# Weight groups of a three-mixer decoder layer in another order, two more weight buffers, another PSUM bank for the narrow group

## The chip, the cores and the metric

The kernel runs on one core of a Trainium2 chip. The metric is the device time of one execution in microseconds (us), the median of the runs. TensorE (PE in the profile) multiplies, VectorE (DVE), ScalarE (ACT) and GpSimd (POOL) do the rest, and SyncE (SP) issues nearly all DMAs from one queue, in the order in which they were written.

## What is computed

One layer of a decoder runs over 288 token columns: 256 of a prompt and 32 of eight short decode sequences. Everything is float32.

```
m = silu(c) @ w_ada + b_ada;  shift, scale, gate = split(m, 3)
h = rmsnorm(x, g_norm) * (1 + scale) + shift
u_a, v_a, z_a, qkv_b, z_b, a_b, b_b, q_c, k_c, v_c, z_c, qi, ki, wi = split(h @ w_in)
y_a = chunk_mlp(gelu(u_a), layernorm(gelu(v_a))) * silu(z_a)      # gMLP
y_b = rmsnorm(gated_delta(conv(qkv_b), a_b, b_b)) * silu(z_b)     # delta rule
y_c = sparse_attention(q_c, k_c, v_c, qi, ki, wi) * silu(z_c)
x = x + gate * (concat(y_a, y_b, y_c) @ w_out);  y = rmsnorm(x, g_final)
```

`D_MODEL` is 4096. `w_ada` (4096 x 12288), `w_in` (4096 x about 15000) and `w_out` (4096 x 4096) are each read once.

## The kernel before

**Groups and units.** `w_in` is cut into 29 groups of 512 columns and one narrow group `c` of 112 columns; `w_out` has 8 groups. `group` makes a list of `Gemm` units of one group, one unit for each 128 rows of the contraction (`kk`). A unit multiplies its 128 x 512 weights with the 128 x 288 tile of h, in four column tiles, each into a PSUM bank of its own (`acc0` to `acc3`, from `acc_tile`). The narrow group has one tile and so used `acc0` alone. To keep float32 accuracy each weight tile is split into `wh` (a cast on ACT) and `wl` (a subtraction on DVE), and h into `hH` and `hL`; each tile of a unit is three matmuls, hH·wh, hL·wh and hH·wl. A full group is 32 units of 12 matmuls, 384 in all; the narrow one 96.

**Loads.** One DMA of 512 KB brings the raw weights of two `Gemm` units into one of four buffers `w` (`N_RAW`). The modulation `m` comes from `Ada` units; each of the first 128 takes two DMAs of 512 KB into buffers `wa` (`N_ADA`, five of them), and eight small matmuls `ada`. The loads stand on SP's queue in the order of the units that need them, so a load that waits for a free buffer holds back all loads behind it.

**First stage.** h isn't known until shift and scale are. `STEPS` cuts the 32 row blocks of h into six steps of two blocks and five of four. In each step the `Ada` units of the next step run between the `Gemm` units of this one; when a step's `ada` sum is complete, `ada_fin1` copies it (`adasb`), transposes it, adds the bias and calls `make_h`, which makes `htmp`, `hH` and `hL`. The groups of the first stage (`SG`: the narrow one, five of attention, and those that `PLAN["p1"]` names) go through all eleven steps, so each step's products are added into SBUF by DVE (`part_finish`; the rows `zb<-zb,acc`). The loop over `lb` spreads `Ada` units among `Gemm` units by a rate that lets each step's `ada` be complete `LEAD` units past its need; for the last step there is nothing past it, so its last `Ada` pair stands directly before its first `Gemm` unit. In a step of two blocks the before has 24 units and a rate of 0.4 `Ada` units each, in the steps 1 to 5; in a step of four 48 units and a rate of 1/3, in the steps 6 to 8.

**Second stage.** `ph2` lists the other groups: those of `PLAN["attn"]`, then the twelve of the delta rule's q, k and v (`C_QKV`), then those of `PLAN["dn3"]`, then v and u of the gMLP (`C_VA`, `C_UA`), then `w_out`. One of the 64 `Ada` units of `gate` stands after every eighth unit. Here h is whole: a gate group (`z_group`) goes from PSUM through `z_fin` into DRAM (`zD`), in one go. The mixers' own chains are Python generators (`dn_all`, `prompt_attn`, `gmlp_prep`, `mix_gen` and others); the `Weaver` puts their instructions between matmuls by its own estimate of times, and `W.finish` writes out all that is left of a chain where the code needs it done. Two such places matter here. `gmlp_open`, before unit 12 (`GMO`) of the last u group, finishes `DN[3]`, the delta rule's fourth and last chain. `need_mix`, before each fourth `w_out` unit of the first output group, finishes `MIX[kb]`: a load `mx` of finished mixer rows from DRAM (`mixD`), its cast `mH` on ACT and its rest `mL` on DVE. The `w_out` units use the K blocks in the order `KB = [2, 3, 4, 5, 6, 7, 0, 1]`; `mixD_160` is block 2, `mixD_165` block 7.

Of the kernel before, what the change touches and what calls it, by code (L numbers as in the profile page):

```python
# [36 lines left out]

GCOL = [512 * i for i in range(22)] + [C_QC + 512 * i for i in range(7)]
FULL = [(0, 128), (128, 128), (256, 128), (384, 128)]
N_RAW, N_ADA, N_SPLIT = 4, 5, 4  # L40
N_BANK = 4
HOP = 0.22
LEAD = 6
BACKLOG = 2.0
CALM = 2.5
NH = 3
LEAD0 = 0
GMO = 12
PAIR = 2
GATE = 8  # L50
GATE0 = 0
GPAIR = 1
STEPS = [(2 * f, 2) for f in range(2 * NH)] + [(4 * f, 4) for f in range(NH, 8)]
PLAN = {"p1": ["zc0", "zc1", "zb0", "zb1", "zb2", "zb3"], "attn": ["za0", "za1"], "dn3": []}


def _size(ap):
# [324 lines left out]
def tile_hybrid_step(ctx: ExitStack, tc: tile.TileContext, I, O):  # L382
# [63 lines left out]
    def w_in(c0):  # L446
        return I["w_in_t"][GCOL.index(c0)]
# [9 lines left out]
    def acc_tile(j):  # L457
        t = psum.tile([P, 512], F32, tag=f"acc{j}", name=f"acc{j}", bufs=1)
        W.bank_use[t.tensor.name] = ("T", 0.0)
        return t  # L460

    class Gemm(Unit):
# [21 lines left out]
        def mm(self, j):  # L484
            us = [self.with_, self] if self.with_ else [self]
            if j == 0 and us[0].first:
                self.st.acc = {}
            off, m = self.tiles[j]
            if us[0].first:
                self.st.acc[j] = acc_tile(j)  # L490
            acc = self.st.acc[j]
            for u in us:
                kk = u.kk
                xh, xl = self.XH[kk // 4][:, kk % 4], self.XL[kk // 4][:, kk % 4]
                a, b = u.wh[:, off:off + m], u.wl[:, off:off + m]
                T.matmul(acc[:m, :NTOK], a, xh, start=u.first, stop=False)
                T.matmul(acc[:m, :NTOK], a, xl, start=False, stop=False)
                T.matmul(acc[:m, :NTOK], b, xh, start=False, stop=u.last)
            if self.last:
                self.finish(j, acc)  # L500
# [265 lines left out]
    def make_h(k0, n):  # L766
# [19 lines left out]
        for c in range(0, n, 2):  # L786
# [12 lines left out]
          ("qc0", w_in(C_QC), FULL), ("qc1", w_in(C_QC + 512), FULL)]  # L799
    SG += [(n, w_in(ZCOL[n][0]), FULL) for n in PLAN["p1"]]  # L800

# [50 lines left out]
    la, lb, la_end = [], [], []  # L852
# [11 lines left out]

    at_, n = [0], la_end[0] + LEAD0
    for us in lb:
        at_.append(at_[-1] + len(us))
    W.units += la[:n]
    i = 0
    while i < len(lb):  # L870
        rate, nxt = max([((min(len(la), la_end[j] + LEAD) - n) / (at_[j] - at_[i]), j) for j in range(i + 1, len(lb))],
                        default=(0, len(lb)))
        us = [u for x in lb[i:nxt] for u in x]
        n0 = n
        for j, u in enumerate(us):
            e = min(len(la), n0 + int(rate * (j + 1)) // PAIR * PAIR)
            W.units += [u] + la[n:e]
            n = e
        i = nxt
# [1337 lines left out]
    def z_group(n):  # L2217
        return group(w_in(ZCOL[n][0]), FULL, ALL, z_fin(ZCOL[n][1]))
# [21 lines left out]
    ph2 = []  # L2240
    for n in PLAN["attn"]:
        ph2 += z_group(n)
    for g in range(4):
        for kind in range(3):
# [5 lines left out]
            ph2 += u  # L2250
    for n in PLAN["dn3"]:
        ph2 += z_group(n)
# [24 lines left out]
    for n in range(2):  # L2277
        u = group(w_in(C_UA + 512 * n), FULL, LAST if n else ALL, uv_finish(UT, 4 * n, y_gen if n else None))
        if n:
            u[GMO].pre.append(gmlp_open)  # L2280
            for i, kb in enumerate(KB[:6]):
# [4 lines left out]
    mixed, n = [], 0  # L2286
    for i, u in enumerate(ph2):
        e = min(len(gates), int((i + 1 - GATE0) / GATE)) // GPAIR * GPAIR
        mixed += [u] + gates[n:e]
        n = max(n, e)  # L2290
# [157 lines left out]
```

## Time and profile before

| | us |
|---|---|
| median of 3 runs | 2605.29 |
| lowest and highest | 2603.06 and 2607.48 |
| the profiled execution | 2601.98 |
| its span, first to last instruction | 2600.3 |
| PE busy | 2498.2 (96%) |
| DVE, ACT, POOL busy | 1622.6, 1055.8, 478.0 |

The first product of h starts at 52.69 us, the second stage at 789 us, the first output group at 2144 us and the last product ends at 2580 us. A matmul's own duration in the trace (about 300 ns) is longer than the distance between two starts, since they are pipelined; the distance is what counts. PEclk is the granted share of TensorE's clock: 1.00 is 2.4 GHz, 0.50 is 1.2 GHz.

### The profile page before, as it was taken

The numbers are of one execution on the slowest core, as the hardware profiler recorded it, in microseconds if no ns is written. First come the engines' busy times: TensorE is split into PE (matmuls) and PEld (weight loads), VectorE is DVE, ScalarE is ACT, GpSimd is POOL, SyncE is SP. The second block draws the span as 40 slices with busy tenths as digits, with TensorE's granted clock in tenths as the row PEclk, the third lists the DMA queues.
The fourth block names the chain that finished last, engine by engine and source line by source line (L and its number), as shares of the span: only waits on it lengthen the run. The fifth ranks groups of instructions, "written<-read, shape, count | busy, mean of one in ns | idle before, by whom it ended". The sixth has DMA issues, their size and how long they took to land. (4 is left out here: it accounts for less than half of the span.)

```text
span 2600.3 us, 51897 instructions
## 1 busy us (share of the span) xinstructions
PE 2498.2 (96%) x19572; PEld 2232.4 (86%) x19572; DVE 1622.6 (62%) x3616; ACT 1055.8 (41%) x2446; POOL 478.0 (18%) x1096
## 2 busy tenths in 40 slices
PE   5999999999999999999999999999999998999997
PEld 3788888888897788888899889989989988999997
DVE  3377765555568798555576576667567566555554
ACT  3423223323344434344444444444454534444443
POOL 1000000000001122534533333443330200000000
PEclk9999999999999999999999999999999999999998
DMA  7988988887656567877776565666666455555554
GB/s 281 369 328 340 343 321 316 314 326 298 220 182 207 169 224 255 284 255 259 252 261 204 171 224 204 203 218 222 200 219 236 143 198 163 188 173 177 177 186 162
DMA packets 207947, 615.88 MB, mean 237 GB/s; under 512 B 41901, under 2 KB 61841, under 8 KB 207697
## 3 DMA queue, kind: packets, MB, share of 16 engines
q1 hardware_dynamic: 196816, 574.82, 62.7%
q0 software_dynamic: 10880, 37.76, 4.2%
q8 instruction: 154, 2.52, 0.4%
q14 instruction: 97, 0.79, 0.1%
HBM read 587.54 MB, written 24.95 MB: 236 GB/s over the span
## 5 line engine op out<-in xcount | busy, mean ns | idle before, releaser
L74 DVE TENSOR_TENSOR wl<-w,wh 128x512 fp32r<-128x512 f32 (+1 forms) x1216 | 801.3, 682 | 672.9 <-ACT wh L74 662.9
L74 ACT CAST wh<-w 128x512 fp32r<-128x512 f32 (+1 forms) x1216 | 712.0, 611 | 1131.7 <-PE acc L74 816.0
L74 PE MATMUL acc<-hH,wh 128*128 128x288 f32 (+1 forms) x3744 | 1151.7, 308 | 20.2 <-ACT hH L74 8.7
L74 PE MATMUL acc<-hH,wl 128*128 128x288 f32 (+1 forms) x3744 | 1109.2, 296 | 1.4 <-DVE wl L74 1.3
L74 PE MATMUL acc<-hL,wh 128*128 128x288 f32 (+1 forms) x3744 | 1109.2, 296 | 0.6 <-DVE hL L74 0.6
L74 PEld LDWEIGHTS acc<-hH,wh 128*128 128x128 f32 (+1 forms) x3744 | 707.0, 189 | 137.7 <-issue 72.1
L74 PEld LDWEIGHTS acc<-hH,wl 128*128 128x128 f32 (+1 forms) x3744 | 708.0, 189 | 5.1 <-DVE wl L74 5.1
L74 PEld LDWEIGHTS acc<-hL,wh 128*128 128x128 f32 (+1 forms) x3744 | 708.5, 189 | 1.3 <-DVE hL L74 1.2
L74 PE MATMUL acc<-mH,wh 128*128 128x288 f32 x1024 | 304.6, 297 | 7.5 <-ACT mH L74 7.5
L74 PE MATMUL acc<-mL,wh 128*128 128x288 f32 x1024 | 302.6, 296 | 0.8 <-DVE mL L74 0.8
L74 PE MATMUL acc<-mH,wl 128*128 128x288 f32 x1024 | 302.8, 296 | 0.0
L74 PEld LDWEIGHTS acc<-mH,wh 128*128 128x128 f32 x1024 | 192.9, 188 | 8.0 <-ACT mH L74 7.7
L74 PEld LDWEIGHTS acc<-mL,wh 128*128 128x128 f32 x1024 | 193.0, 188 | 1.1 <-DVE mL L74 1.1
L74 PEld LDWEIGHTS acc<-mH,wl 128*128 128x128 f32 x1024 | 193.0, 189 | 0.0
L74 PE MATMUL ada<-wa,cT 128*32 128x512 f32 x1024 | 135.3, 608 | 23.9 <-DVE bs L74 18.0
L74 DVE TENSOR_TENSOR zb<-zb,acc 128x288 f32<-128x288 f32 x160 | 70.3, 451 | 43.3 <-PE acc L74 43.0
L74 PEld LDWEIGHTS ada<-wa,cT 128*32 128x32 f32 x1024 | 28.4, 110 | 80.3 <-issue 44.1
L74 POOL TENSOR_TENSOR htmp<-yT,gaT 128x32 f32<-128x32 f32 x20 | 7.8, 388 | 449.0 <-ACT wh L74 335.3
L74 POOL TENSOR_SCALAR frs<-frs 128x1 f32<-128x1 f32 (+1 forms) x3 | 0.9, 297 | 456.0 <-DVE frs L74 455.9
L74 DVE TENSOR_TENSOR R<-R,R 128x248 f32<-128x248 f32 (+30 forms) x248 | 72.7, 293 | 10.4 <-DMA R<-dD 3.9
L74 POOL DMA_INDIRECT vraw<-in_cache_v_dram,ixv x64 | 66.4, 1038 | 42.1 <-issue 13.9
L74 DVE SCALAR_TENSOR_TENSOR cv<-xp,vecs,cv 128x256 f32<-128x256 f32 x144 | 70.9, 492 | 3.6
(443 smaller groups left out, 2342.3 us busy)
## 6 DMA issues: line engine op xcount, KB each, us to landing
w<-in_w_in_t_dram SPq DMA_DIRECT2D x464, 512.0 KB, 4.7
wa<-in_w_ada_t_dram SPq DMA_DIRECT2D x256, 512.0 KB, 6.1
w<-in_w_ada_t_dram SPq DMA_DIRECT2D x128, 512.0 KB, 5.7
w<-in_w_out_t_dram SPq DMA_DIRECT2D x128, 512.0 KB, 3.5
St<-in_state_dn_t_dram SPq DMA_DIRECT2D x16, 512.0 KB, 6.2
out_dram<-St SPq DMA_DIRECT2D x16, 512.0 KB, 3.7
X<-in_x_prompt_dram SPq DMA_DIRECT2D x8, 512.0 KB, 7.1
XF<-in_x_prompt_dram SPq DMA_DIRECT2D x16, 256.0 KB, 5.2
```

What stands on the lines that cost most here:

```text
L74: r = f(*a, **k)
```

## The change

```diff
-N_RAW, N_ADA, N_SPLIT = 4, 5, 4
+N_RAW, N_ADA, N_SPLIT = 4, 7, 4
...
+LAST_LEAD = 8
...
-PLAN = {"p1": ["zc0", "zc1", "zb0", "zb1", "zb2", "zb3"], "attn": ["za0", "za1"], "dn3": []}
+PLAN = {"p1": ["zc0", "zc1", "zb0", "zb1"], "attn": ["zb2", "zb3"], "dn3": ["za0", "za1"]}
...
             if us[0].first:
-                self.st.acc[j] = acc_tile(j)
+
+                self.st.acc[j] = acc_tile(j if len(self.tiles) > 1 else 2)
...
-        rate, nxt = max([((min(len(la), la_end[j] + LEAD) - n) / (at_[j] - at_[i]), j) for j in range(i + 1, len(lb))],
+        rate, nxt = max([((min(len(la), la_end[j] + LEAD) - n) /
+                         (at_[j] - at_[i] - (LAST_LEAD if la_end[j] == len(la) else 0)), j) for j in range(i + 1, len(lb))],
```

Five things change. The first stage has two full groups fewer (`zb2`, `zb3`). They take the place of `za0`, `za1` in front of the delta rule's columns, and `za0`, `za1` (the gMLP's gate) now stand behind the delta rule's columns, in front of v and u. There are seven buffers `wa`. The narrow group accumulates in `acc2`. The last `Ada` pair of the first stage stands eight `Gemm` units earlier. A step of two blocks now has 20 units with 0.48 `Ada` units each (steps 1 to 5), a step of four 40 with 0.4 (steps 6 to 8), so 9.6 and 16 in a step as before.

The order of the instructions shows three of the places. First ACT at the end of the first stage's tenth step, where `hH` of the eleventh is made. Before:

```order
L74 CAST wh<-w 128x112 x4
L74 CAST wh<-w 128x512 x44
L74 CAST wh<-w 128x112 x4
L74 COPY adasb<-ada 128x512
L74 CAST hH_8112<-htmp 128x576 x2
L74 CAST wh<-w 128x512 x26
```

And now:

```order
L75 CAST wh<-w 128x112 x4
L75 CAST wh<-w 128x512 x32
L75 COPY adasb<-ada 128x512
L75 CAST wh<-w 128x512 x4
L75 CAST wh<-w 128x112 x2
L75 CAST hH_6878<-htmp 128x576
L75 CAST wh<-w 128x112 x2
L75 CAST hH_6878<-htmp 128x576
L75 CAST wh<-w 128x512 x26
```

The copy `adasb` has moved ahead of eight weight casts, so units of the tenth step now stand between it and `hH`. On PE, 84 products of the tenth step stand behind the transposes of this `adasb`, where none did.

Second, DVE at the end of the delta rule's last chain; `St` are the states of four heads, `Sup` the products that update them, `oTs` the transposed output. Before, all of it in one piece in front of the gMLP's first instruction (`rep`):

```order
L74 TENSOR_SCALAR R_26175<-R_25755,bsel 128x128 x8
L74 TENSOR_TENSOR wl<-w,wh 128x512
L74 TENSOR_SCALAR R_25755<-R_25755,onr 128x128
L74 SCALAR_TENSOR_TENSOR R_25755<-oTs,vecs,R_25755 128x128
L74 SCALAR_TENSOR_TENSOR St_24190<-St_24190,gls,Sup 128x128 x4
L74 SCALAR_TENSOR_TENSOR St_24191<-St_24191,gls,Sup 128x128 x4
...
L74 SCALAR_TENSOR_TENSOR St_24192<-St_24192,gls,Sup 128x128 x4
L74 SCALAR_TENSOR_TENSOR St_24193<-St_24193,gls,Sup 128x128 x4
L74 COPY rep<-ident 4x32
L74 TENSOR_TENSOR wl<-w,wh 128x512 x3
```

And now:

```order
L75 TENSOR_SCALAR R_24776<-R_24325,bsel 128x128 x8
L75 TENSOR_TENSOR wl<-w,wh 128x512 x2
L75 TENSOR_SCALAR R_24325<-R_24325,onr 128x128
...
L75 SCALAR_TENSOR_TENSOR St_22889<-St_22889,gls,Sup 128x128 x4
L75 TENSOR_TENSOR wl<-w,wh 128x512 x2
L75 SCALAR_TENSOR_TENSOR St_22888<-St_22888,gls,Sup 128x128 x4
L75 SCALAR_TENSOR_TENSOR St_22889<-St_22889,gls,Sup 128x128 x4
L75 TENSOR_TENSOR wl<-w,wh 128x512 x2
L75 SCALAR_TENSOR_TENSOR St_22890<-St_22890,gls,Sup 128x128 x4
L75 SCALAR_TENSOR_TENSOR St_22891<-St_22891,gls,Sup 128x128 x4
L75 TENSOR_TENSOR wl<-w,wh 128x512
```

Weight splits now stand between the state updates, and the gMLP's first instruction comes 750 products of PE behind the last `Sup`.

Third, SP around the start of `w_out`, from the loads of the last u group on. Before:

```order
L74 DMA w<-in_w_in_t_dram 128x1024 x4
L74 DMA w<-in_w_out_t_dram 128x1024
L74 DMA mx<-mixD_160 128x1152
L74 DMA w<-in_w_out_t_dram 128x1024
L74 DMA mx<-mixD_161 128x1152
L74 DMA w<-in_w_out_t_dram 128x1024 x5
L74 DMA out_dram<-vtk 32x1024
L74 DMA mx<-mixD_163 128x1152
L74 DMA w<-in_w_out_t_dram 128x1024 x3
L74 DMA mx<-mixD_162 128x1152
```

And now:

```order
L75 DMA mx<-mixD_161 128x1152
L75 DMA w<-in_w_in_t_dram 128x1024
L75 DMA w<-in_w_out_t_dram 128x1024
L75 DMA mx<-mixD_162 128x1152
L75 DMA w<-in_w_out_t_dram 128x1024 x7
L75 DMA out_dram<-vtk 32x1024
L75 DMA w<-in_w_out_t_dram 128x1024
L75 DMA mx<-mixD_163 128x1152
L75 DMA z_26712<-zD_151 128x288
L75 DMA w<-in_w_out_t_dram 128x1024 x2
L75 DMA z_26838<-zD_151 128x288
L75 DMA w<-in_w_out_t_dram 128x1024
```

Block 4 (`mixD_162`) has moved ahead of eight loads of `w_out` and of block 5 (`mixD_163`); block 5 stands about as many loads down the queue as block 4 did. In PE's order the product that needs block 4 is 194 products behind its load now and 0 before; the one that needs block 5 is 64 behind; the one that needs block 6 is 45 and most of 12 `mix` products behind its load.

## Rows read from the trace of the kernel before

**Rows 1.** The page's first section: busy us of each engine (share of the span).

```profile
PE 2498.2 (96%) x19572; PEld 2232.4 (86%) x19572; DVE 1622.6 (62%) x3616; ACT 1055.8 (41%) x2446; POOL 478.0 (18%) x1096
```

**Rows 2.** Stretches, tile `acc`: us, PE (count), PEld, DVE, ACT, PEclk, DMA share, GB/s.

```profile
112.41:350.08 237.67, 188.55 (x1351) 180.76 (x1351) 98.36 (x225) 0.00 (x0) 1.00 0.88 336
350.08:622.40 272.32, 224.73 (x1621) 216.82 (x1621) 59.33 (x135) 0.00 (x0) 1.00 0.83 318
...
711.90:722.00 10.10, 9.25 (x36) 8.58 (x37) 0.45 (x1) 0.00 (x0) 0.50 0.30 105
2107.43:2111.30 3.87, 3.23 (x9) 2.32 (x9) 0.00 (x0) 0.00 (x0) 0.51 0.61 243
2168.42:2176.00 7.58, 5.42 (x18) 4.41 (x18) 0.00 (x0) 0.00 (x0) 0.50 0.62 207
```

**Rows 3.** Stretches, all instructions; POOL's column comes ahead of PEclk.

```profile
30.00:40.00 10.00, 7.51 (x50) 3.40 (x48) 1.38 (x2) 2.04 (x9) 0.00 (x0) 0.97 0.90 302
70.00:130.00 60.00, 58.49 (x420) 45.67 (x417) 25.46 (x56) 30.39 (x68) 4.07 (x16) 1.00 0.95 368
```

**Rows 4.** PE's waits in the first stage: total us, times, longest.

```profile
PE acc L74 <- DVE v_c L74: 7.4, 7, 1.4
PE ada L74 <- DMA wa<-in_w_ada_t_dram: 1.2, 2, 1.0
```

**Rows 5.** DVE's timeline, end of a step (start, us, what, [idle before <-releaser]).

```profile
703.44 0.46 DVE L74 TENSOR_TENSOR zb<-zb,acc 128x288 f32<-128x288 f32 x1 [0.34 <-PE acc L74]
```

**Rows 6.** PE's timeline at the last step's start.

```profile
703.91 0.29 PE L74 MATMUL acc<-hH,wl 128*128 128x288 f32 x1
704.13 1.93 PE L74 MATMUL ada<-wa,cT 128*32 128x512 f32 x16
706.76 0.66 PE L74 MATMUL ada<-ident,adasb 128*128 128x128 f32 x4 [0.70 <-ACT adasb L74]
711.90 0.58 PE L74 MATMUL acc<-hH,wh 128*112 128x288 f32 x1 [4.48 <-ACT hH L74]
...
716.31 0.58 PE L74 MATMUL acc<-hH,wh 128*128 128x288 f32 x1 [0.64 <-DVE v_c L74]
```

**Rows 7.** PE's timeline at the last delta-rule chain's end, and `Sup` at 1896.

```profile
2095.67 0.29 PE L74 MATMUL acc<-hL,wh 128*128 128x288 f32 x1
...
2096.20 0.29 PE L74 MATMUL acc<-hH,wl 128*128 128x288 f32 x1
2099.67 0.33 PE L74 MATMUL oTs<-ident,R 128*128 128x128 f32 x1 [3.18 <-DVE R L74]
2099.93 7.57 PE L74 MATMUL Sup<-R,R 32*128 32x512 f32 x16
2107.43 0.61 PE L74 MATMUL acc<-hH,wh 128*128 128x288 f32 x1
...
1896.55 1.13 PE L74 MATMUL Sup<-R,R 32*128 32x512 f32 x4
```

**Rows 8.** Timelines of PE, SP and DVE where `w_out` begins.

```profile
2160.63 0.29 PE L74 MATMUL acc<-mH,wl 128*128 128x288 f32 x1
2168.42 0.61 PE L74 MATMUL acc<-mH,wh 128*128 128x288 f32 x1 [7.50 <-ACT mH L74]
2169.81 0.61 PE L74 MATMUL acc<-mL,wh 128*128 128x288 f32 x1 [0.79 <-DVE mL L74]
...
2155.84 6.74 SPq L74 DMA_DIRECT2D w<-in_w_out_t_dram  x3
2162.63 0.43 SPq L74 DMA_DIRECT2D mx<-mixD  x1
...
2168.40 1.36 DVE L74 TENSOR_TENSOR mL<-mx,mH 128x1152 fp32r<-128x1152 f32 x1 [3.78 <-ACT mH L74]
```

**Rows 9.** The tile `mx`: duration ns min/median/max; issue to landing.

```profile
L74 ACT CAST mH<-mx x6: 1133/1152/1157, 2136.7 to 2182.0; 128x1152 fp32r<-128x1152 f32 x6
...
DMA to landing us min/median/max: 3.6/5.5/6.3
```

## Prediction, made before the changed kernel was run

> **What bounds the kernel now.** I read the page first: PE is busy for 2498.2 us, 96% of the span [rows 1], so the reader should take PE as the bound and look for the time in which it stands still or runs slowly. The change leaves the number of products as it is; it can gain only from such time. The stage table tells what a product costs: five products start in 2095.67 to 2096.20, four distances in 0.53 us, 0.133 us each [rows 7]. The steps 1 to 5 of the first stage hold 1350 products (five times 270), or 179.6 us, in 237.67 us, and 48 Ada units, so one of these costs 1.21 us with all that comes with it; the steps 6 to 8 hold 1620 products and 48 Ada units in 272.32 us, which gives 1.18 [rows 2]. I use 1.2. The waits and timelines then show four kinds of lost time: short waits for `v_c` [rows 4], a wait for `hH` [rows 6], a wait for the delta rule's last chain [rows 7] and one for `mH` [rows 8]. After each of the last three PE is granted 0.50 of its clock, its 1.2 GHz level, for about ten us [rows 2], so each costs more than its wait. The second question is what the first stage does to the DMAs, since its steps become shorter while the weights for the modulation stay as many.
>
> **Moved groups, work alone.** Two groups are 768 products, 102 us. They leave the first stage and come back behind it at the same 0.133 us, so the sum for PE is nothing. The additions into SBUF that they no longer need were on DVE behind other work and cost PE nothing. `zb2` and `zb3` stand exactly where `za0` and `za1` stood, with the same evictions and stores, and from there to the third delta-rule chain PE's order is the same, only 768 products earlier. I cost this stretch at nothing. `za0` and `za1` bring eight stores to SP's queue, past the loads of the delta rule's states; at 0.43 us for an issue [rows 8] they fill it for 3.4 of 102 us, so I count nothing, and at most 2 us.
>
> **The narrow group's bank.** Seven waits for `v_c` sum to 7.4 us [rows 4]: the next group's first product waits until DVE has emptied `acc0`. In `acc2` the narrow group itself has to wait for the third tile of the group before it. DVE empties that one from 703.44 to 703.90, and the last product of that group starts at 703.91 [rows 5, 6], so the bank is free just in time; where a weight split stands first on DVE it is late by a fraction of a us. I count 1 us for that over eleven steps, which leaves a gain of 6.4, between 3.4 and 7.4.
>
> **The last Ada pair eight units earlier.** The wait for `adasb` is 0.70 and that for `hH` 4.48, together 5.2 us [rows 6]. Then 36 products take 10.10 us at the low clock [rows 2], where 4.8 would do: 5.3 more, of which 0.6 is the last wait for `v_c`, counted already [rows 6]. That makes 9.9 us. Now 84 products, 11.2 us, stand behind the transposes of `adasb`; the chain from there to the first product took 711.90 − 706.76 = 5.1 us, so 6 us are left over and I count the whole of it. They cover the weight casts that stand ahead of `hH` on ACT now.
>
> **The gate groups behind the delta rule's columns.** The last product ahead of the chain's end ends its turn at 2096.33, the next starts at 2107.43: 11.1 us, in which PE does 16 `Sup` and one transpose. Four `Sup` take 1.13 us where PE runs at full clock, so this work is worth 4.5 + 0.3 us [rows 7], and 6.3 are lost. The 3.87 us behind it run at 0.51 [rows 2], half of which, 1.9, is lost too. Now `Sup` stands among products, and 750 products lie between the last of it and the gMLP's start, so the finishing has nothing to wait for: 8.2 us, at least 6.
>
> **The loads of the mixers' rows.** The third block that `w_out` needs was loaded last: SP issued it at 2162.63, behind three weight loads that waited 6.74 us for buffers, and PE stood for 7.50 and 0.79 us [rows 8]. Behind the first wait come 7.58 us at the low clock [rows 2]; without the 0.79 that is 6.8, half of it lost. Together 11.7 us. Now this block is early, and the next one, block 5, is the late one: 64 products, 8.5 us, after its issue it is needed. It lands after 5.5 us, at most 6.3; its cast takes 1.15 us [rows 9], the rest `mL` 1.36 [rows 8], and in the new order both stand directly ahead of the need. So I expect PE to wait some 2 to 3 us there or at block 6, and take 3, without a fall of the clock: a gain of 8.7, between 0 (the same wait at another block) and 11.7.
>
> **Seven buffers, and what the first stage asks of the DMAs.** At the start the DMAs fell to 302 GB/s for 10 us [rows 3], where buffers were full; two more help by up to 2 us, but PE's order puts 12 more transposes behind the last `ada`. I count nothing. What counts is the rate. A step of two blocks now has 222 products and 9.6 Ada units: 29.5 + 11.5 = 41.0 us, and loads 9 × 0.524 + 0.115 + 19.2 × 0.524 = 14.9 MB, so 363 GB/s. A step of four has 444 and 16: 78.3 us, 26.4 MB, 338 GB/s. In the same way the kernel before asked for 15.95 MB in 47.5 us, 336 GB/s, and that is what it moved [rows 2]; so 336 and 318 were its demand, not a limit, and PE's waits for `wa` were 1.2 us in all [rows 4]. For 60 us, where it asked for more, it moved 368 [rows 3]. Bounds: at 368 nothing is lost; at 336 and 318 the steps take 44.3 and 83.0 us, and 5 × 3.3 + 3 × 4.7 = 31 us are lost. The row where demand was higher is the nearer one, but 363 of 368 leaves no room for loads that come in bursts in one queue, so I take half of what the steps of two blocks would lose at 336, 8 us.
>
> By the Trainium skill, "DMA: Bandwidth & Descriptors", section "Specifications", memory gives one core about 358 GB/s. The row of 368 over 60 us is above that, so this trace does not bear it out as a limit. By it the steps of two blocks would take 41.6 us, 3 us more in all, and the time would be 2575.
>
> **The sum.** −6.4 − 9.9 − 8.2 − 8.7 + 8 = −25.2 us. From the profiled execution's 2602.0 that is 2576.8. That execution lies 3.3 us under the median of its runs; I take the median, 2605.3, and forecast 2580.
>
> **Rivals.** First, the wait for `mH` only moves to block 5 or 6, with its fall of the clock. For it: that load stands as far down SP's queue as the late one did. Against: 8.5 us lie between. The gain of 8.7 is gone: 2589. Second, the first stage gets no more from the DMAs than it did, 336 and 318 GB/s: 2605.3 − 33.2 + 31 = 2603, no change. For it: 363 was held for one stretch of 60 us only. Third, on the other side: more buffers `wa` let SP's queue fill with modulation weights while the few `w` buffers run dry, and the first stage's steps 1 to 8 get less than what they had. All eight load 153.7 MB and take 439.9 us where nothing waits; the gains of 33.2 are used up at 153.7 / 473.1, so below 325 GB/s the kernel is slower than before, and at 310 it takes 2628. Against it: the before did 336 with five buffers. Fourth, the memory's limit above, 358 GB/s, with nothing else lost: 2575. That the change doesn't do what it says is out for the last two places, since the order shows both moved.
>
> **How the numbers follow.** Forecast 0.60, the moved wait 0.16, the held first stage 0.12, the slower one 0.06, the limit at 358 0.06. About 0.2% (5 us) is what a measurement of this kernel can tell from no change. Faster by more: nearly all of the forecast, the moved wait and the limit, a third of the held stage, 0.84. Within: 0.09. Slower: 0.07. The low end takes every gain in full (−7.4 − 9.9 − 8.2 − 11.7), no loss and a little for the start: 2567. The high end takes the moved wait and three quarters of the bound on the DMAs besides: 2600.
>
> **What would show it.** Right: no wait for `v_c` over 0.5 us; no wait and clock 1.00 at the eleventh step's start; `Sup` in pieces among products; block 4's `mH` long done, a wait under 3 us at block 5 or 6; some 355 to 365 GB/s in the steps 1 to 5, with these near 42.5 us each. Wrong: waits of PE for `wa` or `wh` of more than 15 us in the first stage, a new fall of the clock in it, or a wait of 7 us in front of the second `w_out` blocks.

## The result, and the profile of the changed kernel

The changed kernel takes 2577.87 us (median of 4 runs, 2574.68 to 2581.15); the kernel before, on the same chip, 2605.59 (4 runs, 2603.06 to 2607.48). The ratio is 0.9891, 95% interval 0.9873 to 0.9908, so 28 us or 1.1% faster. Three single executions in what follows (one each of the kernel before, b_lead and a_eight) took at least 17% longer than the others and are left out of the ratios. The profiled execution is one of 2580.07 us, with a span of 2578.4; that of before had 2600.3.

Line 1 of the page, beside [rows 1]:

```profile
PE 2490.4 (97%) x19572; PEld 2226.3 (86%) x19572; DVE 1590.0 (62%) x3536; ACT 1056.7 (41%) x2438; POOL 479.0 (19%) x1096
```

PE executes as many instructions as before; DVE lost 80, the additions into SBUF of the two groups that left the first stage. The time must therefore have come from PE's waits and its clock. To see where, I compare the starts of the same products in the two timelines. The program has 14304 products in `acc`; two groups, 768 products or 102.1 us at 0.133 us, have moved, and are taken into account. The boundaries behind the first product are the starts of fixed products, the same in both kernels: the 13th of the second stage, the 196th behind the delta rule's columns, and the first of `w_out`.

| stretch | before, us | after, us | difference without moved work | forecast |
|---|---|---|---|---|
| start to the first product | 52.7 | 48.7 | −4.0 | 0 |
| first stage | 738.4 | 613.8 | −22.5 | −8.3 |
| second stage up to the last delta-rule chain | 1111.9 | 1121.9 | +10.0 | 0 |
| last chain, u and v groups, gate groups | 241.1 | 342.1 | −1.1 | −8.2 |
| output stage to the end | 456.2 | 451.9 | −4.3 | −8.7 |
| span | 2600.3 | 2578.4 | −21.9 | −25.2 |

The sum is near the forecast and the terms are not: the first stage gave more than twice what was expected, and the three places behind it gave little or took. First the first stage, as PE's waits up to 612 us (total us, times, longest):

```profile
PE ada L75 <- DVE bs L75: 18.3, 1, 18.3
PE acc L75 <- ACT hH L75: 4.2, 1, 4.2
PE ada L75 <- DMA wa<-in_w_ada_t_dram: 1.4, 6, 0.2
PE acc L75 <- DVE wl L75: 1.1, 3, 0.6
PE acc L75 <- ACT wh L75: 0.9, 2, 0.7
PE acc L75 <- DVE hL L75: 0.6, 2, 0.4
```

There is no wait for `v_c` or `adasb` any more, and one of the two waits for `hH` is gone [rows 4, 6]; the waits for `bs` and `hH` that are left lie in the start. And the same stretches as in [rows 2, 3], all instructions: the second step alone, the steps 1 to 5, 6 to 8, and the eleventh step (us, then busy us of PE, PEld, DVE, ACT and POOL with counts, granted clock, DMA share, GB/s):

```profile
96.80:138.80 42.00, 41.38 (x311) 32.47 (x307) 28.24 (x65) 12.96 (x23) 2.17 (x8) 1.00 1.01 397
96.80:300.90 204.10, 201.93 (x1518) 161.24 (x1514) 145.65 (x330) 62.76 (x115) 11.71 (x40) 1.00 0.97 370
300.90:530.30 229.40, 229.40 (x1732) 189.85 (x1728) 126.99 (x264) 69.99 (x129) 9.10 (x24) 1.00 0.92 350
600.80:661.00 60.20, 59.80 (x447) 59.58 (x448) 44.41 (x91) 27.73 (x55) 0.00 (x0) 1.00 0.61 190
```

The five steps of two blocks take 204.1 us, 40.8 each, where the prediction had 41.0 without a loss; the steps of four take 76.5, where it had 78.3. The DMAs moved 370 GB/s for 204 us and 397 for one step. The eleventh step runs at clock 1.00 with PE busy for all but 0.4 us.

Behind the first stage PE's timeline has three places to look at (start, us, instruction, tiles, [idle before <-releaser]): the first delta-rule chain's end, a gate group behind the columns, and blocks 5 and 6 of `w_out`.

```profile
1371.60 0.34 PE L75 MATMUL oTs<-ident,R 128*128 128x128 f32 x1 [3.84 <-DVE R L75]
1371.87 3.75 PE L75 MATMUL Sup<-R,R 32*128 32x512 f32 x4
...
1826.03 0.29 PE L75 MATMUL acc<-hH,wl 128*128 128x288 f32 x1
1829.11 0.59 PE L75 MATMUL acc<-hH,wh 128*128 128x288 f32 x1 [2.78 <-DVE zg L75]
...
2150.06 0.40 PE L75 MATMUL acc<-mH,wh 128*128 128x288 f32 x1 [0.42 <-ACT mH L75]
2152.57 0.40 PE L75 MATMUL acc<-mL,wh 128*128 128x288 f32 x1 [2.12 <-DVE mL L75]
```

And their stretches, with the columns of the stretches above:

```profile
1365.00:1396.00 31.00, 24.34 (x92) 14.60 (x91) 18.33 (x67) 13.32 (x58) 13.17 (x37) 0.72 0.28 101
1829.10:1832.50 3.40, 3.39 (x14) 3.40 (x15) 2.54 (x4) 1.24 (x2) 0.00 (x0) 0.51 0.78 245
2153.40:2163.60 10.20, 10.20 (x40) 9.19 (x39) 5.43 (x15) 2.54 (x4) 0.00 (x0) 0.50 0.46 175
```

The reader is to see that a wait of 2.1 us for `mL` stands where the prediction expected 2 to 3, and that ten us at the clock's 1.2 GHz level follow, which it did not expect; that the gate group's eviction is late by 2.8 us; and that the first delta-rule chain ends with hardly a product beside it: 92 instructions in 31 us, clock 0.72. This last place is in the kernel before too, with the same wait at 1489, and the prediction did not speak of it:

```profile
1489.24 0.33 PE L74 MATMUL oTs<-ident,R 128*128 128x128 f32 x1 [3.84 <-DVE R L74]
```

### The profile page after: what moved, and what is told of

The parts are those of the page before. It is cut to its first block, busy times and chain, and to the rows that moved or that the text cites. A ratio compares the mean times of both kernels' runs of the same rounds, so it can differ in the third digit from the quotient of the medians.

```text
span 2578.4 us, 51796 instructions
## 1 busy us (share of the span) xinstructions
PE 2490.4 (97%) x19572; PEld 2226.3 (86%) x19572; DVE 1590.0 (62%) x3536; ACT 1056.7 (41%) x2438; POOL 479.0 (19%) x1096
## 5 line engine op out<-in xcount | busy, mean ns | idle before, releaser
L75 POOL TENSOR_SCALAR tap<-xp,vecs 128x32 f32<-128x32 f32 x144 | 73.0, 507 | 0.4
```

The costliest lines, as they stand in the source:

```text
L75: r = f(*a, **k)
```

## The experiments

All ratios are to the kernel before, run on the same chip; 0.001 is 2.6 us. The kernels ran on several chips, so two of them are compared by their ratios and not by their times.

| kernel | ratio | 95% interval | us against before |
|---|---|---|---|
| changed | 0.9891 | 0.9873 to 0.9908 | −28 |
| b_bank: before, with the bank alone | 0.9993 | 0.9979 to 1.0007 | −2 |
| b_lead: before, with the early Ada pair alone | 0.9965 | 0.9947 to 0.9984 | −9 |
| b_plan: before, with the moved groups alone | 1.0049 | 1.0033 to 1.0066 | +13 |
| a_five: changed, five `wa` buffers | 0.9979 | 0.9965 to 0.9993 | −5 |
| a_six: changed, six | 0.9943 | 0.9923 to 0.9963 | −15 |
| a_eight: changed, eight | 0.9894 | 0.9879 to 0.9909 | −28 |
| a_qclast: changed, one group of qc last in the first stage | 0.9859 | 0.9841 to 0.9877 | −37 |
| a_mx3: changed, three buffers for the mixers' rows | 0.9890 | 0.9876 to 0.9905 | −29 |
| a_zgd: changed, an own buffer for a late gate tile | 0.9879 | 0.9864 to 0.9894 | −32 |
| a_two: changed, all four groups ahead of the delta-rule columns | 0.9842 | 0.9823 to 0.9861 | −41 |
| a_need: changed, mixer rows called for earlier | 0.9884 | 0.9862 to 0.9907 | −30 |
| a_three_need: changed, three groups ahead, with a_zgd and a_need | 0.9846 | 0.9827 to 0.9865 | −40 |

### The parts by themselves

**The bank** (b_bank).

```
-                self.st.acc[j] = acc_tile(j)
+                self.st.acc[j] = acc_tile(j if len(self.tiles) > 1 else 2)
```

> The kernel before with one edit: the narrow group sums in acc2 and no longer in acc0. The prediction's term: seven waits for v_c, 7.4 us, go, and about 1 us comes back as waits for the third tile of the group before; 6.4 us faster than before, between 3.4 and 7.4. Rival: the wait for DVE only changes its place, since the narrow group now waits for the third tile; no change within 2 us, with waits of the narrow group's first products of a similar sum.

Measured: 1.8 us faster, with an interval from 5.5 faster to 1.8 slower. Its waits in the first stage:

```profile
PE acc L74 <- ACT hH L74: 8.7, 2, 4.5
PE acc L74 <- ACT wh L74: 3.8, 4, 1.3
PE ada L74 <- DMA wa<-in_w_ada_t_dram: 2.4, 8, 0.8
PE acc L74 <- DVE wl L74: 1.7, 5, 0.9
```

The 7.4 us for `v_c` are gone; those for `wh` and `wl`, 2.6 and 0.6 in the kernel before, are now 3.8 and 1.7. The first stage became 4.9 us shorter (733.6 for 738.4). In the profiled execution 2.9 us of that are lost at the first delta-rule chain: from the start of `oTs`, behind the same wait of 3.84 us, the same 66 instructions of PE take 24.4 us in before and 27.3 here, with 17.0 and 27.3 us at half clock. The two stretches, before and here:

```profile
1490.00:1513.90 23.90, 20.86 (x66) 11.66 (x65) 14.26 (x52) 8.04 (x33) 8.90 (x27) 0.64 0.31 114
1485.70:1513.00 27.30, 24.21 (x66) 12.92 (x67) 14.27 (x53) 8.05 (x33) 9.59 (x26) 0.50 0.31 109
```

So the term was worth 5 us at its place, and in the end an amount that can't be told from nothing.

**The early Ada pair** (b_lead).

```
-        rate, nxt = max([((min(len(la), la_end[j] + LEAD) - n) / (at_[j] - at_[i]), j) for j in range(i + 1, len(lb))],
+        rate, nxt = max([((min(len(la), la_end[j] + LEAD) - n) /
+                         (at_[j] - at_[i] - (8 if la_end[j] == len(la) else 0)), j) for j in range(i + 1, len(lb))],
```

> The kernel before with one edit: the last Ada pair stands eight units earlier. The prediction's term: the waits for adasb (0.70) and hH (4.48) at the eleventh step go, and the half clock behind them; 9.9 us faster than before. Rival: the chain from the last Ada product to hH is not covered by 84 products and a shorter wait stays, with the same fall of the clock behind it, since before shows such falls behind waits of about 3 us too: 3 to 4 us faster only.

Measured: 9.1 us faster (4.2 to 13.8), the first stage 8.8 us shorter. The waits for `adasb` and the second for `hH` are gone. The term of 9.9 was right.

**The moved groups** (b_plan).

```
-PLAN = {"p1": ["zc0", "zc1", "zb0", "zb1", "zb2", "zb3"], "attn": ["za0", "za1"], "dn3": []}
+PLAN = {"p1": ["zc0", "zc1", "zb0", "zb1"], "attn": ["zb2", "zb3"], "dn3": ["za0", "za1"]}
```

> The kernel before with the plan of groups alone: two delta-rule groups out of the first stage, the gate groups behind the delta-rule columns; five wa buffers, acc0 and the late Ada pair as before. By the prediction's terms 8.2 and 8.7 us are gained and a loss for the DMAs of up to 31 us stands against it, 8 of it expected: 9 us faster. By the trace of the changed kernel: the boundary of the two stages loses 5.6 us and the stretch from there to the last delta-rule chain another 5, the gate stretch gains 1.1 and the output 4.3, so that the plan alone is worth nothing behind the first stage; it is then 5 us slower to 5 us faster, by what the first stage does with five buffers.

Measured: 12.8 us slower (8.6 to 17.2), more than either reading allowed. The first stage is 10.2 us longer than before's without the moved work. With 48 products fewer in a step of two blocks the weights for the modulation must come faster, and five buffers don't deliver them. The next three kernels show that. The three parts add up to 2 us slower, and the changed kernel with five buffers, which has all three, measured 5 faster; the intervals, some 4 us either way for each, allow for that.

### How many buffers

**Five, six and eight** (a_five, a_six, a_eight): the changed kernel with

```
-N_RAW, N_ADA, N_SPLIT = 4, 7, 4
+N_RAW, N_ADA, N_SPLIT = 4, 5, 4
```

and 6 or 8 in the same place.

> The changed kernel with five wa buffers again. The prediction's term for seven buffers: nothing (2 us either way) at the start, and no word on which number the rate of the first stage needs. Trace of the changed kernel: the first matrix product starts 4.0 us earlier and step 0 is shorter by another 5 us than its work explains. If both come from the buffers, this kernel is 4 to 10 us slower than the changed one (2582 to 2588). Rival: the first stage with five buffers keeps no more than the 336 and 318 GB/s of before: up to 31 us slower (2608), with PE's waits for wa above 15 us. Second rival: no difference (2578), the first stage's gain is all in the banks and the lead.

> The changed kernel with six wa buffers. With five it took 2601, with seven 2578, with eight no less. If a load of modulation weights has to be issued early enough to have landed (median 5.9 us) when its Ada unit comes, and each buffer adds the same lead, six lie in the middle: 2585 to 2592. Rival: the seventh buffer is what shifts the places of later tiles, and the number itself counts little: as with five, about 2600. Second rival: six are enough: 2578.

> The changed kernel with eight wa buffers. With five, the steps 0 to 8 of the first stage took 21.7 us more than with seven (53.6, 212.8 and 237.0 us against 48.1, 204.2 and 229.4). If the number of buffers is what limits the Ada units, an eighth gains some more: steps 6 to 8 stand 0.6 us each above the sum of their products and Ada units, so at most 2 to 4 us, 2575. Rival: what counted was the layout or the rate, with seven the loads are early enough: within 2 us of the changed kernel. Second rival: the additional weights in flight push the first stage's own weights back: PE's waits for wh and wl above 5 us, 3 to 6 us slower.

Measured: 2601.08, 2586.92 and 2574.27 us (of eight only the times are used, no trace). By the ratios it is 9 us from five to six, 14 from six to seven, and nothing from seven to eight. Six lies where it was expected, and eight within the 2 us of its first rival; five lost more than was expected and less than its rival said. The first stage with five is 21.8 us longer than with seven, 635.6 for 613.8. Against the same steps of before without the moved work (us):

| steps | 0 | 1 to 5 | 6 to 8 | 9 and 10 | all |
|---|---|---|---|---|---|
| five (a_five) | +0.2 | +7.1 | +3.0 | −11.0 | −0.7 |
| six (a_six) | −4.2 | +2.0 | −0.4 | −11.0 | −13.6 |
| seven (changed) | −5.2 | −1.6 | −4.6 | −11.0 | −22.5 |

The last two steps, where the early Ada pair stands, gain the same with every number. In the steps 1 to 8 seven buffers hold what five lose, and in step 0 they gain 5 us that no term of the prediction had. The start is hardly touched: the first product begins at 49.3 to 53.0 us in the five traces with five buffers, at 49.1 with six, and at 48.3 to 49.4 in the seven traces with seven. Most of the 4.0 us of the first table is the spread of before.

What the buffers do is seen at the weight loads. These rows say who waited for the tile `wa` in the whole span (total us, times), first with five buffers:

```profile
PEld ada L75: 28.9, 30
PE ada L75: 6.1, 15
DMA to landing us min/median/max: 3.3/5.9/10.2
```

and with seven, the changed kernel:

```profile
PEld ada L75: 10.7, 18
PE ada L75: 1.4, 6
```

and in the kernel before:

```profile
PEld ada L74: 16.8, 14
PE ada L74: 5.9, 5
```

Six lie between (PEld 20.7 us in 24 times). From seven to five the products' own waits, PE, grow by 4.7 us only; the waits of PE's weight loads, PEld, by 18.2, and that is most of the 21.8. The steps of four blocks with five buffers:

```profile
315.80:552.80 237.00, 234.76 (x1733) 190.11 (x1729) 127.28 (x264) 69.90 (x129) 9.10 (x24) 1.00 0.90 338
```

338 GB/s, where seven buffers got 350 for the same work in 229.4 us. So the rate did not bound the stage; a load that took a median of 5.9 us to land was issued too late, because its buffer came free too late: in this stretch SP's queue waits 141.1 us for `ada` products to free a buffer, and in that of seven buffers 117.7. In the kernel before, 11.4 of the 16.8 us lie in the start. From the first product on PEld waits for `wa` 5.4 us, 2.3 of them in the steps 1 to 5 and none in the steps 6 to 8, where five buffers have 20.4 in the changed kernel and seven 2.5. So five were nearly enough for the longer steps of before, and are not for the shorter ones.

### The places behind the first stage

**The stage boundary** (a_qclast): one group of qc moved behind the z groups.

```
     SG += [(n, w_in(ZCOL[n][0]), FULL) for n in PLAN["p1"]]
+    SG.append(SG.pop(5))
```

> The changed kernel with the second group of qc's moved behind the z groups in the first stage, so that the z stores are issued before the stage ends. Theory: in the changed kernel DVE's first memset of the second stage lies where the last z tiles lay and waits 4.58 us for their stores; PE's wait for wq (6.1 us) and the half clock of 10.2 us behind it come from that. With the stores done earlier DVE does not wait, the wq wait is 1.4 us as before, and the stretch from the first to the third eighth of the products shrinks from 326.4 to some 319 to 324: 3 to 8 us faster than the changed kernel. Rival: the wait is the setup's own chain (transposes, copies on DVE, wq) and stays at 5 us or more: no change.

In the changed kernel DVE waits at the boundary for the last z stores, with `wq` behind it in its order:

```profile
668.82 0.06 DVE L75 MEMSET sub<- 128x1 f32 x1 [4.58 <-DMA zD<-zb]
...
671.85 0.16 DVE L75 TENSOR_SCALAR wq<-smt 128x32 f32<-128x32 f32 x1
```

With five buffers the same memset ran with no wait, although the program's order is the same:

```profile
686.67 0.06 DVE L75 MEMSET sub<- 128x1 f32 x1
```

That the buffers shift where later tiles lie would explain it; it was not tried by itself. Measured for a_qclast: 8 us faster than the changed kernel by the two ratios (their intervals just touch), as forecast, but not from there. The wait for `wq` is gone and others took its place, 5.4 us for `RL` and 3.4 for `ktk` among them, and the boundary with the attention's first part takes 329.3 us instead of 326.4. The six kernels whose traces show a wait of 5.3 to 6.4 us for `wq`, the changed one among them, take 323.5 to 328.8 us for the same products, mean 325.0; the five with a wait of 1.4 us, before among them, 320.8 to 324.7, mean 323.2; six buffers, with a wait of 2.8 us, 321.5. The difference of the means, 1.8 us, is smaller than the spread within either group, so the wait is not worth the 3 to 8 us of the theory, and the theory fell. What did change is the first delta-rule chain: its `oTs` no longer waits, and products stand beside it:

```profile
1354.92 1.82 PE L75 MATMUL Sup<-R,R 32*128 32x512 f32 x4
1356.67 0.33 PE L75 MATMUL oTs<-ident,R 128*128 128x128 f32 x1
1362.72 1.13 PE L75 MATMUL Sup<-R,R 32*128 32x512 f32 x4
```

In the 60 us around that chain's first `Sup` (from 20 before it to 40 behind) PE stands still for 6.7 us and runs at half clock for 17.0 in the changed kernel; here it is 1.7 and none. At half speed the 17.0 us are worth 8.5, so some 13 us are gained there, an estimate; new falls of the clock at 847 and 1107 us (10.2 and 6.8 us) cost part of it. That the gain comes from this chain fits these numbers and was not tried by itself.

**The place of the gate groups** (a_two).

```
-PLAN = {"p1": ["zc0", "zc1", "zb0", "zb1"], "attn": ["zb2", "zb3"], "dn3": ["za0", "za1"]}
+PLAN = {"p1": ["zc0", "zc1", "zb0", "zb1"], "attn": ["zb2", "zb3", "za0", "za1"], "dn3": []}
```

> The changed kernel with the two gate groups back among the attention's columns, behind the two moved delta-rule groups: all else as changed, so that only the place of the gate groups differs. The prediction's terms for that place are 8.2 us behind the delta-rule columns and, with the loads of the mixers' rows that follow it, some of 8.7: 8 to 15 us slower than the changed kernel. By its trace the forced end of the delta rule is gone, but 4.5 us are lost again at the gate group's fourth eviction and 2 us at waits for R: 1 to 3 us slower only. Rival: none of the place counts, within 1 us.

Measured: 2562.76 us, by the ratios 13 faster than the changed kernel, on the other side of all three expectations. The costs that the prediction named are there again, the waits for the last chain and for block 4:

```profile
PE acc L75 <- ACT mH L75: 7.6, 1, 7.6
...
PE oTs L75 <- DVE R L75: 3.2, 1, 3.2
```

and the stretches, the first delta-rule chain's, the last one's and the output's:

```profile
1320.00:1480.00 160.00, 159.32 (x1298) 145.16 (x1297) 109.14 (x283) 73.44 (x220) 60.37 (x153) 1.00 0.61 204
2050.00:2075.00 25.00, 21.82 (x113) 15.63 (x105) 13.53 (x48) 5.88 (x19) 1.58 (x4) 0.73 0.48 166
2123.40:2137.10 13.70, 7.49 (x28) 6.72 (x28) 7.63 (x15) 4.58 (x8) 0.00 (x0) 0.50 0.64 206
```

The first row is the point: around the first chain PE is busy for 159.3 of 160 us at clock 1.00. With four groups in front of the delta-rule columns products stand beside that chain, and with it goes the stretch of 31 us at clock 0.72: in the 60 us around its first `Sup` PE stands still for 1.0 us and never falls to half clock. The number of groups is not the only way there, since a_qclast has two and covers the chain as well. From the first stage's end to the output's first product this kernel takes 1441.0 us, the changed one 1464.0; the output stage takes 456.6, as in before (456.2).

**The gate group's eviction** (a_zgd).

```
-        zg = tmp288("zg")
+        zg = tl("dnq", [P, NTOK], "zgd", 1) if own else tmp288("zg")
```

where `own` holds for the fourth tile of a group behind the delta-rule columns.

> The changed kernel with a buffer of its own for the fourth gated tile of each of the two late gate groups. Theory: the fourth eviction waits for the store of the second tile (DVE 5.7 us), which stands in SP's queue behind three weight loads that wait for buffers (7.7 us); PE then waits 2.8 us for the bank and runs 3.4 us at half clock. With an own buffer all of it goes: 3 to 5 us faster than the changed kernel. Rival: the next thing late is the weight split queued behind on DVE and ACT; the wait then shows as one for wh or wl, gain under 2 us.

What it was to remove, DVE's and SP's rows of the changed kernel:

```profile
1828.60 0.46 DVE L75 SCALAR_TENSOR_TENSOR zg<-zth,acc 128x288 f32<-128x288 f32 x1 [5.72 <-DMA zD<-zg]
...
1813.43 7.73 SPq L75 DMA_DIRECT2D w<-in_w_in_t_dram  x3
...
1823.37 1.38 SPq L75 DMA_DIRECT2D zD<-zg  x3
```

The stores stand in SP's queue behind three weight loads that wait 7.73 us for buffers; the fourth tile's buffer holds a tile that is not stored yet. Measured: 3 us faster by the ratios, within their intervals. In the trace PE's wait of 2.8 us for `zg` is gone, and so is the half clock behind it, and the stretch of the fourth line of the first table takes 334.5 us instead of 342.1: against before −8.7, where the prediction had −8.2.

**The mixers' rows** (a_mx3, a_need). A third buffer:

```
-        yield from W.slot("mx", 2)
-        mx = tl("gm", [P, 4, NTOK], "mx", 2)
+        yield from W.slot("mx", 3)
+        mx = tl("gm", [P, 4, NTOK], "mx", 3)
```

> The changed kernel with three buffers for the mixers' rows in place of two. Theory: block 5's load is issued too late since it waits for a buffer; with a third one it is issued when the block before it is, PE's waits for mH and mL (0.4 and 2.1 us) go, and with them the half clock of 10.2 us (40 products in it, which cost 5.1 us): 6 to 8 us faster than the changed kernel, and no stretch at half clock between 2140 and 2200 us. Rival: the load stands behind the weight loads in SP's queue and not behind a buffer: the wait only moves to another block, no change. Second rival: the fall of the clock has its own cause and comes without the wait: 2 us faster.

Measured: no difference (0.9890 for 0.9891), so the theory fell. The waits of 0.4 and 2.1 us became 1.7 and 1.0. The load of block 5 was issued at 2135.7 instead of 2137.9, but ACT's rows of the two kernels show that it had landed in both. First the changed kernel:

```profile
2148.00 0.62 ACT L75 CAST wh<-w 128x512 fp32r<-128x512 f32 x1 [0.95 <-PE acc L75]
2148.53 0.43 ACT L75 CAST mH<-uv 128x288 fp32r<-128x288 f32 x1
2148.86 1.15 ACT L75 CAST mH<-mx 128x1152 fp32r<-128x1152 f32 x1
```

and then a_mx3:

```profile
2150.15 0.62 ACT L75 CAST wh<-w 128x512 fp32r<-128x512 f32 x1 [0.99 <-PE acc L75]
2150.68 1.15 ACT L75 CAST mH<-mx 128x1152 fp32r<-128x1152 f32 x1
```

The cast does not wait for the load in either; it stands behind weight casts that each wait for PE. So the next kernel calls for the block three units earlier:

```
-                u[4 * i].pre.append(need_mix(kb))
+                u[4 * i - (3 if 2 < kb else 0)].pre.append(need_mix(kb))
```

> The changed kernel, with each mixer block that is loaded in the output stage called for three units (36 products, 4.8 us) ahead of its first product. With a third buffer the wait for block 5 only went from 2.5 to 2.7 us: its rows had landed, and it is the cast on ACT, which stood behind four weight casts that each waited for PE, that came late. Theory: the cast and the subtraction move ahead of these weight casts, the waits for mH and mL go and the half clock of 10.2 us with them: 5 to 7 us faster than the changed kernel. Rival: ACT now waits for a landing of block 6 or 7 with weight casts behind it, and PE for wh: same or slower.

Measured: 2 us faster than the changed kernel by the ratios, which their intervals can't tell from nothing, and not the 5 to 7 of the theory. In the trace the waits for `mH` and `mL` are gone, a wait of 1.5 us for `wh` is left at block 6, the half clock is 3.4 us long instead of 10.2, and the output stage takes 448.7 us, 3.2 less than in the changed kernel and 7.5 less than before.

**Both ends covered** (a_three_need): `za0` in front of the delta-rule columns, `za1` behind them, with the edits of a_zgd and a_need.

> The changed kernel with one of the two gate groups back in the attention's columns (za0) and one behind the delta-rule columns (za1), the own buffer for its fourth tile, and the mixer blocks called for three units earlier. Theory: the first delta-rule chain, which in the changed kernel ends without products of a matrix beside it (oTs waits 3.84 us, 17 us at half clock behind), gets them again, as with both gate groups in the attention; and one group, 384 products or 51 us, is enough behind the last chain and for the loads of the mixers' rows. So both ends are covered: the 13 us of the kernel with both groups in the attention are kept, its 13.7 us at half clock by the last chain and the wait of 7.6 us for mH with 13.7 us at half clock behind it go: 2545 to 2555. Rival: one group covers neither end in full, and the time is about that of the kernel with both groups in the attention, 2560 to 2565.

Measured: 2564.01 us, a tie with a_two, so the time of the rival and not the 2545 to 2555 of the theory. Its reason does not fit, since the trace shows the two ends covered (the last chain's surroundings and block 5, the second and third row) and the first chain nearly so:

```profile
1320.00:1480.00 160.00, 155.75 (x1243) 139.36 (x1242) 101.13 (x256) 71.86 (x216) 57.06 (x154) 0.99 0.61 204
2020.00:2080.00 60.00, 60.00 (x434) 56.29 (x433) 37.83 (x89) 26.12 (x51) 1.70 (x4) 1.00 0.57 187
2110.00:2160.00 50.00, 48.05 (x347) 46.01 (x346) 39.76 (x83) 24.64 (x48) 0.00 (x0) 1.00 0.57 181
```

Its output stage takes 447.3 us against 456.6, 9.3 less than a_two's. Between the first stage and the output it takes 1448.2 against 1441.0, 7.2 more: 5.3 of it in the attention's first part (328.8 for 323.5), where the executions spread by as much, and the first and second chain wait 2.0 and 2.4 us for `kbT`. Whether the theory fails or the spread hides its last 10 us these runs don't say. Either kernel beats the changed one by some 12 us.

## Why the prediction was right, and where it was not

The time, 2577.87 for 2580, and the sign were right; the sum was made of terms of which several were wrong and cancelled, so its closeness is in part luck. In its order:

- **The base.** The start's 4.0 us and the second stage's +10.0 are no effects of the change that these runs can show: b_bank and b_lead have before's order in the second stage and need 7.4 and 5.4 us more for it than before's profiled execution, and begin 3.3 earlier. With a spread of that size "nothing" stands for the start and the boundary.
- **The narrow group's bank**, −6.4: mis-sized. Alone it is worth 4.9 us in its stage and 1.8 (−1.8 to 5.5) in all. The prediction bounded it from DVE's row alone; the weight splits behind came late instead, by 2.3 us in PE's waits for `wh` and `wl`.
- **The last Ada pair**, −9.9: right, 9.1 alone.
- **Seven buffers and the DMAs**, 0 and +8: this step failed. It took the rate as the question and put the number of buffers at nothing. With five buffers the first stage loses 21.8 us, in size near the 31 of the second rival but at 353 and 338 GB/s and not at 336 and 318; with seven the steps 1 to 8 lose nothing, and step 0 gains 5.2. The waits that were looked at, PE's for `wa`, 1.2 us [rows 4], could not show it, and those of PE's weight loads, 5.4 us from the first product on, hardly: five buffers were short only at the new pace of the Ada units. The price of 1.2 us for one was a little high for a reason of its own. The stretches that it was taken from hold 2.1 and 3.5 us of the waits for `v_c`, which the bank's term takes away; the steps of four blocks come out 1.8 us each below what that price had promised, and 1.2 us of it is this wait. The two groups had to leave the first stage to make room for the buffers: in the program's layout eight z tiles of 288 numbers are 9 KB a partition, two buffers 8, and there is no room for both.
- **The memory limit**, a rival: out, with 370 GB/s over 204 us. The Trainium skill has that too: "Perfetto Trace Analysis", section "Roofline", says that a core whose neighbour is idle can pull more than its share of 358, up to about 120% of it. The trace agrees, with at most 397.
- **The gate groups behind the delta-rule columns**, −8.2: the mechanism was right (8.7 with the eviction mended, 1.1 as it is). What failed is "they fill it for 3.4 of 102 us, so I count nothing", said of the eight stores in SP's queue: SP's time for an issue was counted, and the 7.73 us that loads ahead of them wait for buffers were not.
- **The mixers' rows**, −8.7: 4.3 came. The wait came at block 5, 2.1 us, as expected; that no half clock would follow was wrong (10.2 us of it). And the cause given was wrong: the load had landed, the cast stood late in ACT's order. The prediction's own terms (5.5 us to land, 1.15 and 1.36 for cast and rest, against 8.5 us) leave no wait, so the 2 to 3 us came true by luck. It is the first rival by half.
- **The range.** The high end, by its own words (2589 with 23 us for the DMAs in place of 8), is 2604 and not 2600; the time measured lies far from either.
- **What was not in it.** The costliest place of the second stage, the first delta-rule chain's end, was in before's trace with the same kind of rows as the last one's, and the change leaves it as it is. By the same estimate as above it cost some 15 us (6.9 us of standing still and 17.0 at half clock), against 8.2 for the last chain's end. The three kernels in which products stand beside this chain (a_qclast, a_two, a_three_need) are the fastest of all.

## What to carry to other kernels

A buffer count that is enough at one pace says nothing about a faster one: price it at the demand that the change makes, and look at the waits of the weight loads too, by tile and by stretch, since a late operand showed there (20.4 us from the first product on, with five buffers) far more than at the matmuls (4.1). Price an operation from a stretch that holds none of the waits that another term takes away. Before choosing where to put spare work, list every place where a chain ends with nothing beside it, not only those that the change touches; here the place left alone was worth more than what the change got out of the two that it covered (1.1 and 4.3 us). And an operation with a small duration can still be late by what is queued ahead of it: stores behind loads that wait for buffers, a cast behind casts that wait for PE.

## What the runs showed of the hardware

The DMAs of this one core moved 397 GB/s over 42 us (share 1.01) and 370 over 204 us. The granted clock fell to 0.50 behind waits of 2.1 and 2.8 us, for 10.2 and 3.4 us; behind one and the same wait of 3.84 us, with the same 66 instructions of PE after it, there were 17.0 us at half clock in one kernel and 27.3 in another. The memset of `sub` behind the first stage waited 4.58 us for stores with seven buffers in that stage and not at all with five, in the same order of instructions.
